# A hybrid SSD / gMLP decoder layer on one core: the first six projection tiles run on unnormalised features

## The chip, the cores and the metric

The kernel runs on one core of a Trainium2 chip. The time is the device time of one execution in microseconds (us), and the median of the runs is what counts.

## The reference

One layer of a decoder trunk works on 288 tokens (256 of a prompt and 8 samples of 4) of 2048 features, in float32. It normalises the tokens, projects them with one matrix whose columns are split among two groups of heads (a state-space group, SSD, with a short causal convolution in front of it, and a gated MLP that mixes positions), projects back, and runs a gated feed-forward block and an embedding gate. What the change touches is the beginning:

```python
def rmsnorm(x, g):
    y = xf * lax.rsqrt(jnp.mean(xf * xf, axis=-1, keepdims=True) + EPS)
    return (y * g.astype(jnp.float32)).astype(x.dtype)
...
n = rmsnorm(h, g_mix)
proj = n @ w_in
z, xbc, dt_raw, u, v = ...              # column ranges of proj
xbc_c, conv_new = causal_dwconv(xbc, conv0, conv_w, conv_b)
xbc_c = jax.nn.silu(xbc_c)
...
w = w_s[:, :Q, :Q] * jnp.tril(...)      # spatial weights of the gated MLP, masked
s = jnp.einsum('gts,bcsgd->bctgd', w, vr) + b_s
```

The factor of the norm is one number for each token, the gain `g` one for each feature.

## The kernel before

**Layout.** Features lie on the 128 partitions, tokens along the free axis: an activation is a list of 16 tiles of 128 x 288. A weight tile is 2048 x 128 (16 blocks of 128 x 128, 1 MB) and gives one output tile of 128 x 288 in PSUM. To keep float32 accuracy each operand is split into a high part in a reduced format and a low part, the rest; `mm3` (lines 175 to 181) makes three products for each block: high x high (line 179), low activation x high weight (line 180), high x low (line 181). One such set is called a triple here; a tile takes 16 of them.

**Splits.** `split` makes the two parts of an activation: `hi` on ScalarE with the gain as its scale (line 150), `lo` on VectorE (line 151). `split_w` does it for half a weight tile (8 blocks, 1024 columns): `whi` on ScalarE (line 172), `wlo` on VectorE (line 173), at a raised priority. `load` brings half a tile over SP's queue into one of four `raw` buffers; `whi` and `wlo` have three buffers each. `mtile` loads, splits and multiplies a whole tile into one of three `acc` buffers in PSUM; other results use five `pb` buffers.

**Start.** The features `xin` arrive in eight pieces of 288 KB, half over SP's and half over ScalarE's queue, and behind them the small tables. ScalarE squares each piece (line 239) and TensorE sums over features with a column of ones (`sum_tokens`, line 102). VectorE makes the reciprocal root in twelve small steps (lines 82 to 90), TensorE broadcasts it to all partitions (lines 118 and 120), and VectorE multiplies `xin` by it (line 249). Only then are the features split into `n_act`, which stays for all projection tiles. Tiles 0 to 2 are multiplied together, k by k, into `ps01`, with the narrow dt projection beside them (line 257, its weights `gw` multiplied by the gain at line 243).

**After it.** The loop at the end goes over four groups g of the SSD heads, with six convolution tiles each; for g = 0 these are the tiles 0 to 5. `dt_work` and `decay_work` turn the dt projection into decay factors when tile 0 is done. `conv_tile` copies a PSUM tile into `cbuf` on ScalarE (lines 331 and 332), and runs the convolution on both engines (lines 336 to 343); `cbuf` has three buffers, the others two. In groups 1 to 3, z tiles come between, and `advance` emits pieces of `ssd_group` of the group before. When the last group has ended, `mlp_pools` reuses its memory: GpSimd's queue loads the residual `h` again and then the spatial weights and biases, and line 576 multiplies the weights by the triangular mask `T1`. The sixteen tiles of the first part of the output projection follow, each added to `h` at line 707, then the rest of the v tiles, then `spatial` as a side job of the u tiles, which uses the masked weights in `mix` (line 597).

**Order.** The instructions are written in program order, and a scheduler at build time fixes the order on each engine from dependences, priorities (program order, but for the raised ones) and its own estimate of times; it may take a step far ahead of its place when its inputs are there. On the chip each engine then runs its list in that order.

## Time and profile before

| | us |
|---|---|
| median of 3 runs | 1802.67 (1802.15 to 1803.92) |
| the profiled execution | 1801.47 |
| its span in the trace | 1799.3 |
| TensorE busy | 1765.1 (98%) |
| VectorE busy | 1062.1 (59%) |
| ScalarE busy | 826.9 (46%) |

PE is TensorE, PEld its weight loads, DVE VectorE, ACT ScalarE, POOL GpSimd, SP SyncE. The granted clock of TensorE is given as a share of 2.4 GHz; 0.50 is its lower level, 1.2 GHz. A float32 matmul is recorded as two instructions. "Idle before" is the time for which an engine stood still just before an instruction, and after the arrow stands what it waited for. A busy TensorE is not one at its peak: only the clock and the count of products tell how fast it moves on.

### The profile page before, as it was taken

The numbers are of one execution on the slowest core, as the hardware profiler recorded it, in microseconds if no ns is written. First come the engines' busy times: TensorE is split into PE (matmuls) and PEld (weight loads), VectorE is DVE, ScalarE is ACT, GpSimd is POOL, SyncE is SP. The second block draws the span as 40 slices with busy tenths as digits, with TensorE's granted clock in tenths as the row PEclk, the third lists the DMA queues.
The fourth block names the chain that finished last, engine by engine and source line by source line (L and its number), as shares of the span: only waits on it lengthen the run. The fifth ranks groups of instructions, "written<-read, shape, count | busy, mean of one in ns | idle before, by whom it ended". The sixth has DMA issues, their size and how long they took to land.

```text
span 1799.3 us, 31672 instructions
## 1 busy us (share of the span) xinstructions
PE 1765.1 (98%) x13084; PEld 1731.5 (96%) x13084; DVE 1062.1 (59%) x1655; ACT 826.9 (46%) x1432; POOL 31.2 (2%) x79
## 2 busy tenths in 40 slices
PE   8999999998999999999999999999999999999996
PEld 7989988978999999999999999999999999999996
DVE  3768687776445686555555554444555555554665
ACT  3585758463345544444333333333333333444452
POOL 0001010101000000000000000000000000000000
PEclk6999999999999999999999999999999999999998
DMA  4536464627555544554555545555555455555452
GB/s 161 180 132 230 133 216 143 223 88 267 165 164 165 165 135 162 165 165 158 167 164 166 165 165 159 166 163 171 167 164 168 163 168 167 161 167 169 164 166 89
DMA packets 83600, 297.63 MB, mean 165 GB/s; under 512 B 9488, under 2 KB 9616, under 8 KB 83200
## 3 DMA queue, kind: packets, MB, share of 16 engines
q1 hardware_dynamic: 75600, 268.85, 46.3%
q0 software_dynamic: 6128, 23.34, 3.6%
q10 hardware_dynamic: 1728, 3.43, 0.5%
q8 instruction: 102, 1.67, 0.4%
q14 instruction: 42, 0.34, 0.1%
HBM read 283.19 MB, written 12.39 MB: 164 GB/s over the span
## 4 chain that ended last, share of the span: by engine, by line
PE 75%; DVE 0%; ACT 0%; DVEq 0%; issue 0%
PE acc L179 25%; PE acc L181 24%; PE acc L180 24%; PE pb L597 0%; PE pb L181 0%; PE pb L179 0%; PE pb L180 0%; PE pb L589 0%; DVE h L829 0%; PE pb L102 0%; PE pb L118 0%; DVE wlo L173 0%; DVE h L707 0%; PE pb L120 0%; DVEq L916 0%
## 5 line engine op out<-in xcount | busy, mean ns | idle before, releaser
L179 PE MATMUL acc<-hi,whi 128*128 128x288 f32 x4000 | 1187.5, 297 | 7.7 <-DVE h L707 4.4
L180 PE MATMUL acc<-lo,whi 128*128 128x288 f32 x4000 | 1184.9, 296 | 0.0
L181 PE MATMUL acc<-hi,wlo 128*128 128x288 f32 x4000 | 1181.0, 295 | 1.2 <-DVE wlo L173 1.2
L172 ACT CAST whi<-raw 128x1024 fp32r<-128x1024 f32 (+1 forms) x516 | 533.7, 1035 | 827.8 <-PE acc L180 664.8
L173 DVE TENSOR_TENSOR wlo<-raw,whi 128x1024 fp32r<-128x1024 f32 (+1 forms) x516 | 623.3, 1208 | 486.2 <-ACT whi L172 479.5
L179 PEld LDWEIGHTS acc<-hi,whi 128*128 128x128 f32 x4000 | 753.1, 188 | 11.7 <-issue 7.3
L181 PEld LDWEIGHTS acc<-hi,wlo 128*128 128x128 f32 x4000 | 755.0, 189 | 3.7 <-DVE wlo L173 1.8
L180 PEld LDWEIGHTS acc<-lo,whi 128*128 128x128 f32 x4000 | 753.8, 188 | 1.5 <-issue 0.6
L783 DVE SCALAR_TENSOR_TENSOR Up<-acc,rs 128x288 f32<-128x288 f32 x44 | 20.1, 457 | 41.9 <-PE acc L181 41.9
L778 DVE TENSOR_TENSOR G<-acc,rs 128x288 f32<-128x288 f32 x44 | 20.1, 457 | 41.6 <-PE acc L181 41.6
L338 DVE SCALAR_TENSOR_TENSOR cva<-cbuf,cwh,cva 128x312 f32<-128x312 f32 x72 | 38.5, 538 | 1.3 <-ACT cva L336 0.4
L551 ACT ACTIVATE gt<-gt 128x288 f32<-128x288 f32 x32 | 14.2, 443 | 40.5 <-DVE gt L550 40.5
L389 ACT ACTIVATE xw<-xdt,dec 128x64 f32<-128x64 f32 x96 | 24.4, 338 | 5.9 <-DVE xdt L386 5.9
L102 PEld LDWEIGHTS pss<-ones,sq 128*128 128x128 f32 x96 | 20.6, 333 | 3.9 <-ACT sq L239 3.9
L102 PE MATMUL pss<-ones,sq 128*128 128x1 f32 x96 | 20.6, 352 | 3.7 <-ACT sq L239 3.7
L418 DVE TENSOR_TENSOR h<-h,pb 128x512 f32<-128x512 f32 x32 | 20.9, 680 | 1.1 <-PE pb L417 1.1
L366 ACT ACTIVATE Rh<-cst,dtAh 128x128 fp32r<-128x128 f32 x64 | 20.6, 397 | 1.5 <-PE pb L371 1.5
L784 DVE TENSOR_TENSOR Up<-Up,G 128x288 f32<-128x288 f32 x44 | 20.2, 458 | 1.5
L366 ACT ACTIVATE Rl<-cst,dtAl 128x128 fp32r<-128x128 f32 x64 | 20.8, 399 | 0.0
L424 DVE TENSOR_TENSOR h<-h,decS 128x512 f32<-128x512 f32 x32 | 20.1, 683 | 0.0
L780 DVE SCALAR_TENSOR_TENSOR G<-Gt,G 128x288 f32<-128x288 f32 x44 | 19.9, 453 | 0.1
L779 ACT ACTIVATE Gt<-G 128x288 f32<-128x288 f32 x44 | 19.4, 441 | 1.2 <-DVE G L778 1.2
(270 smaller groups left out, 927.0 us busy)
## 6 DMA issues: line engine op xcount, KB each, us to landing
raw<-in_wa_dram SPq DMA_DIRECT2D x416, 512.0 KB, 3.6
raw<-in_wd_dram SPq DMA_DIRECT2D x64, 512.0 KB, 3.5
raw<-in_wd_dram SPq DMA_DIRECT2D x32, 384.0 KB, 3.1
h<-in_h0T_dram POOLq DMA_DIRECT2D x16, 512.0 KB, 6.6
out_dram<-h POOLq DMA_DIRECT2D x16, 512.0 KB, 5.9
h<-in_xT_dram POOLq DMA_DIRECT2D x4, 576.0 KB, 7.1
raw<-in_wple_dram SPq DMA_DIRECT2D x4, 512.0 KB, 3.6
xin<-in_xT_dram ACTq DMA_DIRECT2D x4, 288.0 KB, 6.0
```

Source lines behind the costliest of these rows:

```text
L102: nc.tensor.matmul(ps[:, c:c + 1], lhsT=acc[:, t:t + P], rhs=ones[:, 0:1], start=first and c == 0, stop=last and c == 2)
L172: nc.scalar.copy(a, r)
L173: nc.vector.tensor_sub(b, r, f32(a))
L179: nc.tensor.matmul(ps, lhsT=wh, rhs=hi, start=first, stop=False)
L180: nc.tensor.matmul(ps, lhsT=wh, rhs=lo, start=False, stop=False)
L181: nc.tensor.matmul(ps, lhsT=wl, rhs=hi, start=False, stop=last)
L338: nc.vector.scalar_tensor_tensor(ao, cb[:, j:j + NCO], wt[j], ao, op0=ALU.mult, op1=ALU.add)
L366: nc.scalar.activation(cols(r, i), T1, AF.Identity, scale=f32(d[:, c, k + i:k + i + 1]))
L389: nc.scalar.activation(xw[:, 64 * h:64 * h + 64], xd[:, 64 * h:64 * h + 64], AF.Identity, scale=dec[:, c, 8 * g + h:8 * g + h + 1])
L418: nc.vector.tensor_add(h0[q][:, i], h0[q][:, i], ps)
L424: nc.vector.tensor_mul(r3(hh, 64), r3(hh, 64), bc_in(decS[:, 2 * q + i, hs], 64))
L784: nc.vector.tensor_mul(u, u, G)
```

## The change

The first six tiles (group 0) are multiplied from `x_act`, the split of the features with the gain but without the norm. Since the norm is a factor of each token, it is applied to the output: `conv_tile` gets `rs0` and multiplies by it on VectorE as it copies from PSUM into `cbuf`, instead of the copies on ScalarE; `dt_work` does the same. The weights of tiles 0 to 2 are loaded and split in quarters (512 columns) in the order in which they are used, interleaved with `xin`; their second halves get buffers of their own in the start pool. The tables move from SP's and ScalarE's queues to GpSimd's, `vec` to the head of ScalarE's. The sums of squares are added up on VectorE (`sqa`), and TensorE sums once over features at the end (`rstd_compact`). Then `xin` is multiplied by the norm and split into `n_act` as before, for the tiles from group 1 on. The convolution's buffers move to a pool of their own, which is opened before the start pool. The multiplication of the spatial weights by the mask moves from `spatial_weights` into `spatial`, behind the reciprocal root `rv`.

```diff
@@ -211,6 +211,8 @@
     warm = small([P, 1], "warm")
     nc.gpsimd.memset(ones, 1.0)
     nc.scalar.activation(warm, ones[:, 0:1], AF.Exp)
+    cv_pool = tc.tile_pool(name="conv", bufs=1)
+    cvp = cv_pool.__enter__()
     start = tc.tile_pool(name="start", bufs=1)
     s0 = start.__enter__()
     xin = [s0.tile([P, 2, NT], F32, name=f"xin{q}") for q in range(8)]
@@ -223,39 +225,67 @@
     for _ in range(14):
         nc.tensor.matmul(wu[:, 0:P], lhsT=ones, rhs=ones, start=True, stop=True)
 
+    raws = {(m, j): st.tile([P, 1024], F32, tag="raw", name="raw", bufs=4) for j in range(2) for m in range(3)}
+
+    def first_w(m, j):
+        nc.sync.dma_start(raws[m, j // 2][:, 512 * (j % 2):512 * (j % 2) + 512],
+                          wa[m, :, 4 * j:4 * j + 4].rearrange("p k m -> p (k m)"))
+
+    nc.scalar.dma_start(vecs, vec)
     for q in range(8):
-        (nc.scalar if q % 2 else nc.sync).dma_start(xin[q], xT[:, 2 * q:2 * q + 2])
-    nc.sync.dma_start(vecs, vec)
-    nc.scalar.dma_start(csts, cst)
-    first = {(m, 0): load(wa[m, :, 0:8], 8) for m in range(3)}
-    nc.scalar.dma_start(wdts, wdt)
-    nc.scalar.dma_start(dtals, dtal)
-    nc.scalar.dma_start(scv, sconv)
-
-
-    pss = big("pss")
-    for q in range(8):
-        sq = s0.tile([P, 2, NT], F32, tag="sq", name="sq", bufs=4)
-        nc.scalar.activation(sq, xin[q], AF.Square)
-        for j in range(2):
-            sum_tokens(pss, sq[:, j], first=q + j == 0, last=q + j == 8)
-    halves = {at: split_w(raw, 8) for at, raw in first.items()}
-    nc.vector.tensor_mul(gw, wdts, bc_in(vecs[:, V_MIX:V_MIX + 16], 32))
-    rs0 = bcast_tokens(rsqrt_compact(pss[:, 0:3], 2048.0, EPS, "rm"), keep_psum=True)
-    n_act = []
+        (nc.scalar if q < 4 else nc.sync).dma_start(xin[q], xT[:, 2 * q:2 * q + 2])
+        if q % 2 == 0:
+            for m in range(3):
+                first_w(m, q // 2)
+    nc.gpsimd.dma_start(wdts, wdt)
+    nc.gpsimd.dma_start(csts, cst)
+    nc.gpsimd.dma_start(dtals, dtal)
+    nc.gpsimd.dma_start(scv, sconv)
+
+
+    def quarter(m, j):
+
+        if j % 2 == 0:
+            if j == 0:
+                w = [st.tile([P, 1024], F32R, tag=t, name=t) for t in ("whi", "wlo")]
+            else:
+                w = [s0.tile([P, 1024], F32R, name=f"{t}{m}") for t in ("whi", "wlo")]
+            halves[m, j // 2] = w
+        c = slice(512 * (j % 2), 512 * (j % 2) + 512)
+        w_hi, w_lo = halves[m, j // 2]
+        raw = raws[m, j // 2]
+        nc.scalar.copy(w_hi[:, c], raw[:, c])
+        nc.vector.tensor_sub(w_lo[:, c], raw[:, c], f32(w_hi[:, c]))
+
+    halves = {}
+    x_act, n_act = [], []
     ps01 = [big("ps01")[:, 0:NT] for _ in range(2)] + [pa.tile([P, NT], F32, tag="acc", name="acc")]
     pdt = big("pdt")
     for q in range(8):
+        for k in (2 * q, 2 * q + 1):
+            xk = xin[q][:, k % 2]
+            x_act.append(split(xk, gain=vcol(V_MIX, k)))
+            for m in range(3):
+                if k % 4 == 0:
+                    quarter(m, k // 4)
+                mm3(ps01[m], halves[m, k // 8], k % 8, x_act[k], k == 0, k == KD - 1)
+    nc.vector.tensor_mul(gw, wdts, bc_in(vecs[:, V_MIX:V_MIX + 16], 32))
+    for k in range(KD):
+        nc.tensor.matmul(pdt[32 * (k % 4):32 * (k % 4) + 32, 0:NT], lhsT=gw[:, k], rhs=xin[k // 2][:, k % 2],
+                         start=k < 4, stop=k >= 12, tile_position=(0, 32 * (k % 4)))
+
+    sqa = s0.tile([P, 2, NT], F32, name="sqa")
+    for q in range(8):
+        sq = sqa if q == 0 else s0.tile([P, 2, NT], F32, tag="sq", name="sq", bufs=1)
+        nc.scalar.activation(sq, xin[q], AF.Square)
+        if q:
+            nc.vector.tensor_add(sqa, sqa, sq)
+    nc.vector.tensor_add(sqa[:, 0], sqa[:, 0], sqa[:, 1])
+    rs0 = bcast_tokens(rstd_compact(sqa[:, 0], 2048.0, EPS, "rm"))
+    for q in range(8):
         nc.vector.tensor_mul(xin[q], xin[q], bc_mid(rs0, 2))
         for k in (2 * q, 2 * q + 1):
-            xk = xin[q][:, k % 2]
-            n_act.append(split(xk, gain=vcol(V_MIX, k), tags=LONG))
-            for m in range(3):
-                if (m, k // 8) not in halves:
-                    halves[m, 1] = split_w(load(wa[m, :, 8:16], 8), 8)
-                mm3(ps01[m], halves[m, k // 8], k % 8, n_act[k], k == 0, k == KD - 1)
-            nc.tensor.matmul(pdt[32 * (k % 4):32 * (k % 4) + 32, 0:NT], lhsT=gw[:, k], rhs=xk,
-                             start=k < 4, stop=k >= 12, tile_position=(0, 32 * (k % 4)))
+            n_act.append(split(xin[q][:, k % 2], gain=vcol(V_MIX, k), tags=LONG))
     nc.vector.tensor_scalar_mul(cwh, vecs[:, V_CB:V_CB + 120], 0.5)
 
     dt = small([P, 3, 32], "dt")
@@ -269,7 +299,7 @@
     decS = small([P, 8, 32], "decS")
     def dt_work():
         df = s0.tile([P, 384], F32, name="dtf")
-        nc.scalar.copy(df[:, 0:NT], pdt[:, 0:NT])
+        nc.vector.tensor_mul(df[:, 0:NT], pdt[:, 0:NT], rs0)
         nc.vector.tensor_copy(r3(df[:, NT:384], 32), bc_mid(df[:, 256:288], 3))
         pd = big("pd")
         for c in range(3):
@@ -322,14 +352,17 @@
     def samples(ap):
         return ap[:, 259:NCV].rearrange("p (b t) -> p b t", t=7)[:, :, 0:4]
 
-    def conv_tile(i, ps):
-        sd = sd_box["pool"]
-        cb, a, t = (sd.tile([P, NCV], F32, tag=n, name=n, bufs=b) for n, b in (("cbuf", 3), ("cva", 2), ("cvt", 2)))
+    def conv_tile(i, ps, rs=None):
+        cb, a, t = (cvp.tile([P, NCV], F32, tag=n, name=n, bufs=b) for n, b in (("cbuf", 3), ("cva", 2), ("cvt", 2)))
         nc.gpsimd.memset(cb[:, 0:3], 0.0)
         nc.scalar.copy(cb[:, 259:NCV].rearrange("p (b t) -> p b t", t=7)[:, :, 0:3], scv[:, i])
         new = cb[:, 259:NCV].rearrange("p (b t) -> p b t", t=7)[:, :, 3:7]
-        nc.scalar.copy(cb[:, 3:259], ps[:, 0:256])
-        nc.scalar.copy(new, r3(ps[:, 256:288], 4))
+        if rs is None:
+            nc.scalar.copy(cb[:, 3:259], ps[:, 0:256])
+            nc.scalar.copy(new, r3(ps[:, 256:288], 4))
+        else:
+            nc.vector.tensor_mul(cb[:, 3:259], ps[:, 0:256], rs[:, 0:256])
+            nc.vector.tensor_mul(new, r3(ps[:, 256:288], 4), r3(rs[:, 256:288], 4))
         ao, to = a[:, 0:NCO], t[:, 0:NCO]
         o = slab(name="cvo")
         wt = [cwh[:, 24 + 4 * i + j:25 + 4 * i + j] for j in range(4)]
@@ -573,13 +606,13 @@
         nc.gpsimd.dma_start(wss, wsS)
         nc.gpsimd.dma_start(w, wsT)
         nc.gpsimd.dma_start(b.rearrange("p a b -> p (a b)"), bsP[0:1].partition_broadcast(P))
-        nc.vector.tensor_mul(w, w, bc_mid(T1, KD))
         return bss, wss, w, b
 
     def spatial(nv, mp, bss, wss, w, b):
         vS = vS_box[0]
         sS = sS_box[0] = mp.tile([P, KD, 32], F32, name="sS")
         r = rstd_compact(nv.acc, 2048.0, 4.0 * EPS, "rv")
+        nc.vector.tensor_mul(w, w, bc_mid(T1, KD))
         vts = {}
 
         def to_tokens(g):
@@ -646,6 +679,7 @@
     def mlp_pools():
 
         sd_pool.__exit__(None, None, None)
+        cv_pool.__exit__(None, None, None)
         hp = ctx.enter_context(tc.tile_pool(name="hp", bufs=1))
         h = hp.tile([P, KD, NT], F32, name="h")
         mlp = tc.tile_pool(name="mlp", bufs=1)
@@ -669,7 +703,7 @@
         tiles = [16 + g, 20 + g] + list(range(4 * g, 4 * g + 4))
         zs = []
         for j, i in enumerate(tiles):
-            ps = ps01[at] if at < 3 else mtile(wa[at], n_act)
+            ps = ps01[at] if at < 3 else mtile(wa[at], n_act if g else x_act)
             if at == 0:
                 dt_work()
                 start.__exit__(None, None, None)
@@ -678,7 +712,7 @@
                 decay_work()
                 decay_sample()
             at += 1
-            conv_tile(i, ps)
+            conv_tile(i, ps, None if g else rs0)
             advance(1)
             if g and j in (1, 2, 4, 5):
                 zs.append(z_tile(mtile(wa[24 + 4 * (g - 1) + len(zs)], n_act)))
```

## Rows read from the trace of the kernel before

**Rows 1.** The page: TensorE's busy time, and the chain that ended last by engine

```profile
PE 1765.1 (98%) x13084; PEld 1731.5 (96%) x13084; DVE 1062.1 (59%) x1655; ACT 826.9 (46%) x1432; POOL 31.2 (2%) x79
...
PE 75%; DVE 0%; ACT 0%; DVEq 0%; issue 0%
```

**Rows 2.** Stretches: us, busy time and count by engine, granted clock, DMA share, GB/s

```profile
5.00:10.00 5.00, 2.21 (x11) 2.02 (x10) 0.00 (x0) 0.00 (x0) 0.00 (x0) 1.00 1.05 403
...
15.00:20.00 5.00, 5.00 (x25) 5.00 (x25) 2.45 (x2) 3.25 (x6) 0.00 (x0) 0.50 0.77 267
...
40.00:50.00 10.00, 10.00 (x83) 8.96 (x75) 7.94 (x19) 3.50 (x9) 0.00 (x0) 0.95 0.01 2
```

**Rows 3.** Timeline of the start: start us, duration, engine, line, operation, count, idle before

```profile
10.91 20.64 PE L102 MATMUL pss<-ones,sq 128*128 128x1 f32 x96 [3.69 <-ACT sq L239]
...
11.14 0.22 DVE L259 TENSOR_SCALAR cwh<-vec 128x120 f32<-128x120 f32 x1 [11.14 <-DMA vec<-in_vec_dram]
...
35.50 5.41 DVE L249 TENSOR_TENSOR xin<-xin,pb 128x576 f32<-128x576 f32 x8 [1.58 <-PE pb L120]
...
36.88 0.85 PE L179 MATMUL ps<-hi,whi 128*128 128x288 f32 x2 [1.42 <-ACT hi L150]
...
37.90 3.78 PE L257 MATMUL pdt<-xin,gw 128*32 128x288 f32 x32
...
41.61 0.40 PE L180 MATMUL ps<-lo,whi 128*128 128x288 f32 x1
```

**Rows 4.** Stretches, line 179 alone: the first product of each triple, counted

```profile
40.00:60.00 20.00, 11.64 (x41) 7.53 (x42) 0.97 0.33 110
...
60.00:80.00 20.00, 11.61 (x38) 7.77 (x38) 0.91 0.61 211
...
80.00:90.00 10.00, 7.40 (x26) 4.68 (x26) 1.00 0.47 172
```

**Rows 5.** DMA issues: KB each, median us from issue to landing

```profile
xin<-in_xT_dram ACTq DMA_DIRECT2D x4, 288.0 KB, 6.0
...
wsr<-in_wsT_dram POOLq DMA_DIRECT2D x1, 1024.0 KB, 12.6
```

**Rows 6.** Groups of instructions, 36 to 62 us: busy us, mean ns, idle before

```profile
L151 DVE SCALAR_TENSOR_TENSOR lo<-xin,vec,hi 128x288 fp32r<-128x288 f32 x16 | 7.0, 512 | 0.0
...
L249 DVE TENSOR_TENSOR xin<-xin,pb 128x576 f32<-128x576 f32 x8 | 5.4, 750 | 1.6 <-PE pb L120 1.6
```

**Rows 7.** Groups of VectorE's instructions, 50 to 100 us

```profile
L173 DVE TENSOR_TENSOR wlo<-raw,whi 128x1024 fp32r<-128x1024 f32 x15 | 18.3, 1221 | 12.8 <-ACT whi L172 12.8
...
L338 DVE SCALAR_TENSOR_TENSOR cva<-cbuf,cwh,cva 128x312 f32<-128x312 f32 x21 | 11.1, 537 | 0.7 <-ACT cva L336 0.4
...
L288 DVE SCALAR_TENSOR_TENSOR dtwt<-dtwt,dtws 128x96 f32<-128x96 f32 x7 | 1.8, 255 | 0.1
```

**Rows 8.** Timeline of TensorE, 68 to 72 us: the decay matmuls, first and last

```profile
68.34 0.33 PE L301 MATMUL pdec<-dtA,cst 128*128 128x64 f32 x2
...
69.94 1.97 PE L313 MATMUL pdec<-dtA,cst 32*128 32x32 f32 x16
```

**Rows 9.** Stretches, all engines: the first half of group 1

```profile
100.00:150.00 50.00, 50.00 (x365) 43.27 (x365) 37.70 (x70) 36.52 (x108) 1.39 (x5) 1.00 0.37 124
```

**Rows 10.** Timeline of VectorE, 432 to 436 us

```profile
432.09 2.29 DVE L576 TENSOR_TENSOR wsr<-wsr,cst 128x2048 f32<-128x2048 f32 x1 [5.00 <-DMA wsr<-in_wsT_dram]
...
434.30 1.18 DVE L707 TENSOR_TENSOR h<-h,acc 128x288 f32<-128x288 f32 x3
```

**Rows 11.** Stretches, line 179 alone: around the stop at 430 us

```profile
430.00:434.00 4.00, 0.00 (x0) 0.00 (x0) 0.95 0.66 275
...
434.00:438.00 4.00, 1.67 (x4) 1.28 (x4) 0.50 0.13 14
...
438.00:441.00 3.00, 1.88 (x6) 1.34 (x5) 0.59 0.75 246
```

**Rows 12.** TensorE's waits: us in total, times, longest us

```profile
PE acc L179 <- DVE h L707: 4.4, 1, 4.4
```

## Prediction

> **What bounds the kernel now.** I read the page's busy times first [rows 1]: TensorE is busy 1765.1 us of a span of 1799.3 us, and the chain that ended last is three quarters TensorE, nearly all of it the three products of each weight tile (lines 179 to 181). So time is won only where TensorE is idle or does work that the change drops. The table of stretches [rows 2] and the timeline of the start [rows 3] show where that is. The 48 sums of squares (96 records, line 102) hold TensorE from 10.91 us for 20.64 us; with the norm's own steps the first product is issued at 36.88 us, the 32 dt products (line 257) take the next 3.78 us, and only from 41.61 us do products run back to back. TensorE's clock is 0.50, its 1.2 GHz level, for most of this, although the engine is 100% busy from 15 to 20 us: being busy with one-column matmuls did not raise it. To follow position rather than busy time I count the first products of each triple (line 179; 16 a tile) by stretch [rows 4]. The 3 issued before 40 us [rows 3] and the 41 and 38 of the next two stretches of 20 us make 44 by 60 us and 82 by 80 us; 26 follow in 10 us. So the 48th (tiles 0 to 2) falls at 61.6 us, the 96th (start of tile 6) at 85.4 us, and a triple costs about 0.40 us, a tile 6.4 us. A second stop stands at 430 us (below).
>
> **Part 1: products from raw features.** Tiles 0 to 2 no longer wait for the norm. Their first product needs `vec`, `xin0` and three weight quarters, about 1.2 MB, and their splits. The DMAs moved 403 GB/s from 5 to 10 us [rows 2] and an `xin` piece landed 6.0 us after issue with eight in flight [rows 5]. I put the first triple at 8 us: 6 us if the first pieces land alone, 11 us if everything issued beside them (xin1 to 3, more quarters, and 1 MB of tables) lands together.
>
> Two hardware queues filled that stretch at 403 GB/s with all DMA engines busy (share 1.05), so a third queue cannot add bandwidth to it. The Trainium skill's page "DMA: Bandwidth & Descriptors", section "Issuing engines are not separate DMA queues", says the same and speaks against moving `wdt`, `cst`, `dtal` and `scv` to GpSimd's queue: they interleave with the pieces that the first product needs. By that rule my 8 us would be up to 2.6 us later (an estimate, 1.05 MB at the row's 403 GB/s).
>
> All 6.6 MB are in by about 19 us at that rate, counted from 2 to 3 us. The 48 triples take 48 x 0.40 = 19.2 us if TensorE is never short. Its suppliers: VectorE makes 16 `lo` in 7.0 us [rows 6] and 12 `wlo` quarters; a quarter, half of the 1.22 us of a 1024-wide one [rows 7], is 0.65 us with its fixed part, 7.8 us in all; 14.8 us together, below 19.2, and ScalarE the same. So TensorE sets the pace from 8 us to 27 us. I add 2 us for products at the low clock (0 to 5: a stretch at half clock costs half of itself): tiles 0 to 2 end at 29 us, 27 to 34.
>
> Behind them, on TensorE: the dt products, 3.8 us, which before filled a wait and now stand in the path; token sum and broadcast, 12 small matmuls at 0.12, 1.4 us (16 such take 1.97 us, [rows 8]). Then tiles 3 to 5, 19.2 us, and the dt and decay matmuls, 0.7 us (6 at 0.12) and 3.6 us (from 68.34 to 71.91, [rows 8]), which stood ahead of the 96th triple before too. Without any wait for another engine the 96th triple falls at 29 + 5.2 + 19.2 + 4.3 = 57.7 us, against 85.4.
>
> **Part 2: what VectorE must have done by then.** Tile 5 needs the PSUM buffer of tile 2, and so `rs0` and tile 2's eviction, now on VectorE; tile 6 needs tile 3's buffer and the first normalised features. In the order of the program the list is: main loop 14.8; `gw` 0.7; seven adds of squares and the fold, 5.1 (as a 576-wide product, 0.68); the reciprocal root 2.4 (twelve steps of three columns, 0.2 each, an estimate below the 0.25 of 96 columns); eight products with the norm 5.4 and 16 `lo` 7.0 [rows 6]; seven `wlo` of tiles 3 to 6 at 1.22, 8.5; four evictions of two instructions, 0.6 each, 2.4. That is 46.3 us. `dt_work` adds about 6 (23 small steps at 0.25, [rows 7]), and one convolution, whose buffer tile 3's eviction takes (three cyclic `cbuf`), 3 x 0.54 + 0.6 = 2.2: 54.5 us. From a start at 7 us without a gap this ends at 61.5 us; with 10% of gaps at 67 us. The squares and the adds fit into VectorE's spare 4 us of the main loop only in part. So VectorE, not TensorE, sets tile 6: 58 us if small steps and convolutions come late, 74 us if dt and three more convolutions are queued ahead and gaps are 10%. I take 62 us, nearest to the list without gaps. Gain at the 96th triple: 85.4 - 62 = 23 us (11 to 28). Evictions wait for `rs0`, and behind them on VectorE stand the `wlo` of the next tile and the first `lo` of tile 6; TensorE waits for both. The fall to half clock that such a wait brings is not added: before had one too, inside the 85.4.
>
> After tile 6 VectorE is some five convolutions, 11 us, behind its old position. From 100 to 150 us it was busy 37.7 of 50 us [rows 9], a slack of 12 us; three accumulators and three `cbuf` allow about that lag. I take 1 us of loss (0 to 5). If that slack were not there, up to 11 us would come back.
>
> **Part 3: covers.** ScalarE loses two eviction copies a tile and gains 16 `hi`; it stays beside the path, hidden by VectorE's longer list. The sixteen raw splits take 32 of 38 slabs until tile 5 ends and the six convolution outputs the other 6; no other slab is asked for in this group, so this costs nothing; a seventh claim would hold VectorE until tile 5 ends. On SP's queue the second halves of tiles 1 and 2 reuse two of the four `raw` buffers, so their quarters, and `xin5` to `xin7` behind them, wait until the first halves of tiles 0 and 1 are split, at about 11 us by the pace above. TensorE reaches the ninth k (their first use) at 8 + 8 x 1.2 = 17.6 us, and a landing takes up to 6 us [rows 5]: 0, to 3 us if it is late. The tables on GpSimd's queue come ahead of the states that `ssd_group` loads there much later, which wait for the start pool anyway: 0.
>
> **Part 4: the spatial mask.** Before, VectorE sat 5.0 us for `wsr` and then worked 2.29 us on the mask, with the adds of line 707 queued behind [rows 10]; the transfer took 12.6 us to land [rows 5]. TensorE ran at half clock after it [rows 11] and had waited 4.4 us for that add [rows 12]: 4 triples in the 8 us from 430 us where 20 fit. 6 more of 7.5 followed to 441 us [rows 11], so the stop cost 17.5 x 0.40 = 7 us. The mask is now issued after `rv`, behind the adds in program order, and its first use lies behind the sixteen output tiles and the rest of the v tiles. Even hoisted by the build's scheduler it stands behind the adds that are ready. Gain 7 us (0 to 7.5). In its new place it costs 2.3 us of VectorE's time beside TensorE: 0, or up to 2 if it delays the first `vt`.
>
> **Sum.** 23 - 1 + 7 = 29 us. Against the profiled execution, 1801.47 us (1799.3 of span and 2.2 around it): 1772.5. The median of the runs is 1.2 us above that execution: 1773.7, call it 1773.
>
> **The rivals.**
> Norm and convolutions first: VectorE's queue puts dt and convolutions ahead of tile 2's and 3's eviction, and tile 6 starts at 70 to 74 us with another fall of the clock. For it: in the old trace the eight norm products ran as one block from 35.50 us, ahead of every `lo` [rows 3]. Gain 9 to 14 in front, 16 to 21 in all: 1782 to 1787.
> Full cover: the squares hide in the main loop and the evictions come in time. Gain 27 and 7: 1766 to 1769.
> The mask does not move: the build's scheduler fills the same hole with it, since nothing but its transfer holds it back (in the old trace `cwh`, line 259, ran at 11.14 us, far ahead of its place, [rows 3]). The adds stay behind it: no 7 us, 1780.
> Slower: the start stays at 1.2 GHz. The clock stayed 0.50 through 100% busy stretches [rows 2], and after the stop at 430 us too it was 0.50 [rows 11]. If products arrive in small groups between waits for quarters, evictions and `rs0`, each triple costs 0.3 us more (about 0.7 us there, from 434.9 to 438 us, against 0.40). The Trainium skill's page "TensorE: Matmul & The Clock Gate", section "HAM oscillation — how this bites in real kernels", describes that: bursts between waits keep falling back to the low clock. The gain of 29 us is used up after 29 / 0.3 = 97 triples at the low clock, that is if tiles 0 to 5 all run so; with two tiles more (32 triples, 10 us) the time is 1812. Against it: at half clock a triple takes 0.7 us, longer than its supplies (0.3 us of VectorE's time), so products become dense, and dense products got 0.95 from 40 us on [rows 2].
>
> **How the numbers follow.** Forecast (1768 to 1780) 0.50; norm first 0.20; full cover 0.12; mask unmoved 0.10; slower 0.06; the rest, within 0.2%, where losses later eat the gain, 0.02. The range runs from the full cover with the first triple at 6 us and no low clock (2 us each, and 1 of rounding: 1761) to norm first with 4 us of the lag in group 1 given back (1791); outside are the slower case and the rest. A difference under 0.2% (3.6 us) can't be told from none here. Faster 0.92, same 0.02, slower 0.06.
>
> **What would show it.** In the new trace: first product at 6 to 11 us; the 48th triple near 29 us, the 96th near 62 us; VectorE over 90% busy from 10 to 65 us; a wait of TensorE on the new eviction into `cbuf` or on a `lo`; no wait on line 707's add near 400 us. It is wrong if the 96th triple is later than 74 us, if the clock stays 0.50 after 15 us, or if group 1 shows new waits on VectorE of over 5 us.

## The result, and the profile after

The median is 1785.37 us (1783.51 to 1786.97) against 1802.41 us (1801.66 to 1803.92) for the kernel before in the same runs: a ratio of 0.9904, 95% interval 0.9887 to 0.9921, 17.0 us faster. The forecast was 29 us faster; the time lies inside the range. The profiled execution of after took 1786.97 us, the slowest of its four, with a span of 1785.2 us: 14.1 us below the span of before, so the traces account for a little less than the medians.

The page of after, against [rows 1]: TensorE's busy time fell by 14.0 us, VectorE's rose by 13.0 us.

```profile
PE 1751.1 (98%) x12994; PEld 1713.6 (96%) x12994; DVE 1075.1 (60%) x1698; ACT 831.6 (47%) x1442; POOL 33.4 (2%) x83
...
PE 76%; DVE 0%; ACT 0%; DVEq 0%; issue 0%
```

Both kernels work through the same tiles in the same order, so a place in the work has a time in each. Place n is the start of the first product number 16 n (line 179, counted from 0). From place 6 on that is where tile n starts, as long as tiles have sixteen triples; the last row is a count alone. Up to place 5 the tiles run into one another (0 to 2 are multiplied k by k, and tile 3 begins among them), so there a place is a number of triples and not a tile. The table has the time of some places in each trace and the difference: what has been won up to there.

```
place    before    after   won
  0        36.9      8.1   28.8
  3        61.7     37.3   24.3
  5        79.6     52.2   27.4
  6        86.0     67.6   18.4
  9       107.7     86.9   20.8
 10       114.5     98.8   15.7
 17       175.0    161.3   13.7
 40       371.4    357.6   13.8
 46       434.9    420.7   14.2
 50       463.4    450.1   13.3
250      1755.6   1741.0   14.6
```

Three things are to be read from it. The products from raw features win 28.8 us at once; between places 5 and 6 a stop takes 9 us back; and from tile 17 on hardly anything moves any more, though the forecast had 7 us to come at tile 46. What goes between tiles 6 and 17 are for the most part the decay matmuls and the low clock after them, which before stood ahead of place 5 and now stand ahead of tile 10 (the last sixteen of them at 93.81 us, in place of the 69.94 of [rows 8]). The 18.4 us won at tile 6 thus hold some 5 us that are only put off.

The stretches of the start of after, with the columns of [rows 2]: us, busy time and count of PE, PEld, DVE, ACT and POOL, granted clock, DMA share, GB/s.

```profile
5.00:10.00 5.00, 2.32 (x14) 1.91 (x14) 1.96 (x5) 2.57 (x5) 0.00 (x0) 0.86 1.04 401
10.00:15.00 5.00, 5.00 (x19) 2.62 (x18) 4.59 (x9) 4.36 (x10) 0.00 (x0) 0.50 1.05 388
15.00:20.00 5.00, 5.00 (x35) 3.74 (x34) 4.93 (x11) 5.00 (x14) 0.00 (x0) 0.96 1.05 389
...
30.00:35.00 5.00, 5.00 (x40) 5.00 (x40) 2.25 (x3) 0.51 (x1) 0.00 (x0) 1.00 0.81 231
35.00:40.00 5.00, 5.00 (x40) 5.00 (x40) 1.95 (x12) 0.00 (x0) 0.00 (x0) 1.00 0.27 102
40.00:45.00 5.00, 5.00 (x41) 5.00 (x40) 1.27 (x2) 1.45 (x2) 0.00 (x0) 1.00 0.06 12
45.00:50.00 5.00, 5.00 (x40) 5.00 (x39) 5.00 (x8) 4.71 (x10) 0.00 (x0) 1.00 0.24 93
50.00:55.00 5.00, 2.60 (x20) 2.29 (x18) 5.00 (x16) 5.00 (x11) 0.00 (x0) 1.00 0.00 0
55.00:60.00 5.00, 2.33 (x10) 2.20 (x11) 5.00 (x12) 1.76 (x9) 0.00 (x0) 0.64 0.18 40
60.00:65.00 5.00, 5.00 (x29) 5.00 (x29) 4.98 (x11) 1.06 (x1) 2.12 (x4) 0.68 0.76 246
```

VectorE (third pair) is nearly full from 10 to 30 us, as forecast; then it works 5.5 of 15 us, while TensorE runs at its best; and from 45 us on VectorE is full and TensorE stands still for 5 of 10 us. What VectorE waits for in the hole shows in its timeline: start us, duration, engine, line, operation, count, and in brackets the idle time before it.

```profile
27.54 0.45 DVE L283 TENSOR_TENSOR sqa<-sqa 128x288 f32<-128x288 f32 x1
...
36.51 0.16 DVE L82 TENSOR_SCALAR rmx<-pb 128x3 f32<-128x3 f32 x1 [4.26 <-PE pb L102]
...
38.68 0.16 DVE L90 SCALAR_TENSOR_TENSOR rmy<-rmt,rmy 128x3 f32<-128x3 f32 x1
42.51 1.22 DVE L173 TENSOR_TENSOR wlo<-raw,whi 128x1024 fp32r<-128x1024 f32 x1 [3.66 <-ACT whi L172]
44.95 5.44 DVE L286 TENSOR_TENSOR xin<-xin,rs 128x576 f32<-128x576 f32 x8 [1.22 <-ACT rs L125]
```

On TensorE the two small steps of the norm's chain stand here:

```profile
35.75 0.72 PE L102 MATMUL pb<-ones,sqa 128*128 128x1 f32 x6
...
43.73 0.61 PE L118 MATMUL pb<-cst,rmy 128*128 128x128 f32 x4
```

The fold of the squares ends at 27.99 us, but the sum over features runs at 35.75; the root ends at 38.84, but its broadcast runs at 43.73. Both had their input for 5 to 8 us. TensorE was busy with products of the first tiles in between: the two steps stand behind these in its list, where the build's scheduler put them. So the norm products begin at 44.95 us.

TensorE's longest waits in after, for all of the span: us in total, times, longest.

```profile
PE pd L306 <- DVE dtf L303: 3.4, 1, 3.4
PE acc L181 <- DVE wlo L173: 3.2, 3, 1.5
PE acc L179 <- DVE h L741: 3.1, 1, 3.1
```

The first and half of the second are the stop at 52 us. The third is the wait of [rows 12], line 707 then and line 741 now: the stop at 430 us, which the moved mask was to remove, is still there. VectorE's timeline at that place:

```profile
417.87 2.29 DVE L615 TENSOR_TENSOR wsr<-wsr,cst 128x2048 f32<-128x2048 f32 x1 [3.73 <-DMA wsr<-in_wsT_dram]
420.08 1.18 DVE L741 TENSOR_TENSOR h<-h,acc 128x288 f32<-128x288 f32 x3
```

It is the pair of [rows 10] once more: the mask, whose new place in the program comes up some 180 us later (at 599 us, as an experiment below shows), has been put back directly ahead of the adds.

### The profile page after: what moved, and what is told of

Same layout as the page of the kernel before. It is cut to its first block, busy times and chain, and to the rows that moved or that the text cites. A ratio compares the mean times of both kernels' runs of the same rounds, so it can differ in the third digit from the quotient of the medians.

```text
span 1785.2 us, 31566 instructions
## 1 busy us (share of the span) xinstructions
PE 1751.1 (98%) x12994; PEld 1713.6 (96%) x12994; DVE 1075.1 (60%) x1698; ACT 831.6 (47%) x1442; POOL 33.4 (2%) x83
## 4 chain that ended last, share of the span: by engine, by line
PE 76%; DVE 0%; ACT 0%; DVEq 0%; issue 0%
PE acc L179 25%; PE acc L181 25%; PE acc L180 24%; PE pb L630 0%; PE pb L179 0%; PE pb L181 0%; PE pb L180 0%; PE pb L102 0%; PE pb L622 0%; DVE h L863 0%; PE pb L118 0%; DVE wlo L173 0%; DVE h L741 0%; PE pb L120 0%; DVEq L950 0%
## 5 line engine op out<-in xcount | busy, mean ns | idle before, releaser
L172 ACT CAST whi<-raw 128x1024 fp32r<-128x1024 f32 (+1 forms) x510 | 528.3, 1037 | 829.9 <-PE acc L180 657.6
L173 DVE TENSOR_TENSOR wlo<-raw,whi 128x1024 fp32r<-128x1024 f32 (+1 forms) x510 | 615.6, 1208 | 469.4 <-ACT whi L172 462.7
L157 DVE TENSOR_TENSOR lo<-Up,hi 128x288 fp32r<-128x288 f32 x44 | 19.9, 452 | 0.0
L156 ACT CAST hi<-Up 128x288 fp32r<-128x288 f32 x44 | 19.1, 434 | 1.2 <-DVE Up L818 0.5
```

The source lines that it names most:

```text
L172: nc.scalar.copy(a, r)
L173: nc.vector.tensor_sub(b, r, f32(a))
```

## The experiments

**The mask: moved line or moved work.** Does the line's new place do anything, and what is it worth when the mask really runs late? In the first kernel only the line is moved, in the kernel before.

```diff
-        nc.vector.tensor_mul(w, w, bc_mid(T1, KD))          # in spatial_weights
         r = rstd_compact(nv.acc, 2048.0, 4.0 * EPS, "rv")
+        nc.vector.tensor_mul(w, w, bc_mid(T1, KD))          # in spatial
```

> The kernel before with one part of the change alone: the product of the spatial weights with the mask is written behind the reciprocal root rv, nothing else. Theory: the line changes its place in the text, but nothing but its own transfer holds it back, so the scheduler at build time puts it back ahead of the adds of the output projection. Then TensorE waits about 4.4 us for those adds as before, and the time is that of before, 1802 us, within 0.2%. Rival (the prediction's part 4): the adds go first, TensorE does not stop, 7 us less, 1795 us.

Measured: 1803.4 us against 1802.66, ratio 1.0004 (0.9994 to 1.0014). VectorE's timeline of this run has the mask and the adds where they were:

```profile
431.02 2.29 DVE L582 TENSOR_TENSOR wsr<-wsr,cst 128x2048 f32<-128x2048 f32 x1 [4.13 <-DMA wsr<-in_wsT_dram]
433.23 1.18 DVE L707 TENSOR_TENSOR h<-h,acc 128x288 f32<-128x288 f32 x3
```

The second kernel is after with a mask that needs a value made from the root `rv` (a factor of 1), so that it cannot run before it.

```diff
-        nc.vector.tensor_mul(w, w, bc_mid(T1, KD))
+        keep = small([P, 1], "keep")
+        nc.vector.tensor_scalar(keep, r[:, 0:1], 0.0, 1.0, op0=ALU.mult, op1=ALU.add)
+        nc.vector.scalar_tensor_tensor(w, w, keep, bc_mid(T1, KD), op0=ALU.mult, op1=ALU.mult)
```

> The changed kernel, with the masked product made to depend on rv by a factor of 1 worked out from it, so that it cannot run before rv is there (about 600 us). Theory: the stop of TensorE at 413 us in the changed kernel is still the mask's wait for its weights on VectorE, with the adds queued behind it; without it 3.1 us of waiting and about 3 us at half clock go, 5 to 7 us in all: 1779 us against 1785. Rival: the adds then wait for something else that is as late (the residual h lands at about the same time as the weights, or a weight split is late): under 2 us of gain.

Measured: 1779.58 us (1777.10 to 1781.00), ratio 0.9870 (0.9855 to 0.9885). The adds run as soon as their tile is done, and the mask at 599 us:

```profile
416.65 1.18 DVE L743 TENSOR_TENSOR h<-h,acc 128x288 f32<-128x288 f32 x3 [2.90 <-PE acc L181]
...
599.39 2.34 DVE L617 SCALAR_TENSOR_TENSOR wsr<-wsr,keep,cst 128x2048 f32<-128x2048 f32 x1
```

What has been won at tile 50 rises from 13.3 to 19.0 us; 0.3 of the 5.7 was there at tile 40. A line moved alone did nothing; the dependence is worth 5.8 us by the medians.

**The stop at tile 6: order or amount of VectorE's work.** VectorE's list after 44.95 us has the norm products and the sixteen `lo` ahead of the first convolutions. This kernel is after with the norm products and the splits written behind the dt work and the first four convolutions (the decay work moves along).

```diff
+    def norm_acts():
         for q in range(8):
             ...
             if at == 0:
                 dt_work()
+            if at == 4:
+                norm_acts()
                 start.__exit__(None, None, None)
```

> The changed kernel, with the eight products with the norm and the sixteen splits of the normalised features written after the third tile's convolution and the dt work, not before them, so that VectorE has the dt copy and the low weight part of tile 5 ahead of most of the splits. Theory A (order): TensorE's stop from 52 to 58 us comes from two small steps that stand behind eleven splits on VectorE; with them ahead, the stop and the half clock after it go, and 5 to 8 us are won: 1778 to 1780 us. Theory B (VectorE is late as a whole, because it stood idle for about 9 us between 32 and 45 us while the norm's sum and broadcast waited in TensorE's list): the stop moves to tile 6, whose accumulator or features come no earlier, and the gain is 0 to 2 us.

Measured: 1789.53 us (1788.48 to 1791.09), ratio 0.9927 (0.9913 to 0.9942), 4 us slower than after, which neither theory had. The stop at 52 us is gone and another has come, as theory B had it; tile 6 starts at 67.5 us, as in after:

```profile
67.51 0.58 PE L179 MATMUL acc<-hi,whi 128*128 128x288 f32 x1 [8.13 <-ACT cvo L376]
```

The arrow names a copy on ScalarE; the second eviction of tile 3 ended 0.15 us before the product (more on that below). Behind the longer stop the clock is 0.50 from 65 to 70 us, where after has 1.00, and at tile 20 12.3 us are won in place of 13.8. So this other order does not bring tile 6 forward. The next two kernels take work and waits away. The first leaves out the squares, the sum, the root and the broadcast, and takes the norm's factor as 1.

```diff
-    sqa = s0.tile([P, 2, NT], F32, name="sqa")
-    ...
-    rs0 = bcast_tokens(rstd_compact(sqa[:, 0], 2048.0, EPS, "rm"))
+    rs0 = slab(name="rs", tag="rs")
+    nc.gpsimd.memset(rs0, 1.0)
```

> The changed kernel without the squares, their sum, the reciprocal root and the broadcast: the norm's factor is a constant 1, set at the start. What is left out is the value of the first norm. It takes away VectorE's idle time of 9 us between 32 and 45 us, and 5.6 us of adds and 2.4 us of the root on VectorE. Theory B (VectorE is late as a whole): the 96th triple comes 12 to 15 us earlier, at 53 to 56 us, and the time is 1770 to 1773 us. Theory A (order alone): the copy of dt and the weight part still stand behind the splits, TensorE stops as before, and no more than the 5.6 us of adds is won: 1779 us or more.

Measured: 1774.55 us (1772.08 to 1777.85), ratio 0.9845 (0.9830 to 0.9860). Tile 6 starts at 55.1 us, as theory B had it, and 27.8 us are won at tile 20; the time is 1.6 us above theory B's range and far below theory A's. The second keeps the squares and their additions and leaves out only sum, root and broadcast:

```diff
-    rs0 = bcast_tokens(rstd_compact(sqa[:, 0], 2048.0, EPS, "rm"))
+    rs0 = slab(name="rs", tag="rs")
+    nc.gpsimd.memset(rs0, 1.0)
```

> The kernel after with the squares and their eight additions kept, but the sum over features, the root and the broadcast left out: the norm's factor is the constant 1, so the output is that of unscaled features. It tells the two halves of what the norm costs VectorE at the start apart: the additions (7 by 0.75 us and one of 0.45, 5.7 us) and the idle time (4.3 us in front of the root, 3.7 in front of the weight rests and 1.2 in front of the norm products, 9 us). Theory 'idle time': tile 6's first product comes at 55 to 60 us (without any of the norm's chain it came at 55.1, in the kernel after at 67.6) and the time is 1774 to 1778 us. Theory 'work': the additions are what costs, tile 6 comes at 61 to 67 us and the time is 1780 to 1785 us.

Measured: 1774.02 us (1772.98 to 1777.33), ratio 0.9849 (0.9832 to 0.9865); tile 6 at 57.8 us, 22.1 us won at tile 20. The place of tile 6 speaks for the idle time. The median lies in that theory's range too, but by help of something else: the scheduler put the mask behind the first adds here, at 412.90 us, so that 27.3 us are won at tile 50 (28.2 without the additions), and without these 5 us the time would fall between the two theories. At tile 20 the 14.0 us between after and the kernel without the norm's chain fall apart into 5.7 us, as much as the additions take on VectorE, and 8.3 us for sum, root and broadcast, near VectorE's 9.1 us of idle time in its three holes. Of the 8.3 us, 2.0 are there at place 3 already, ahead of the holes' effect on tile 6. The 8.3 us are also more than waiting: the root's twelve steps take VectorE 2.3 us, and with the factor known from the start the norm products, the evictions (from 42.33 us on in place of 50.68) and the dt steps run earlier too. So the chain of sum, root and broadcast costs at least as much as the additions; how much of it is the wait for TensorE alone these runs do not separate.

**Can the chain be made shorter on VectorE?** The next kernel has the late mask and a root on all partitions: one matmul with a 128 x 128 matrix of ones, the root's steps 288 wide, no broadcast.

```diff
-    rs0 = bcast_tokens(rstd_compact(sqa[:, 0], 2048.0, EPS, "rm"))
+    tot = big("tot")[:, 0:NT]
+    nc.tensor.matmul(tot, lhsT=ones, rhs=sqa[:, 0], start=True, stop=True)
+    rx, rt = sqa[:, 1], slab(name="rt", tag="ta")
+    ...                              # the root's steps, 288 wide
```

> The kernel after with the mask truly late (as in the run mask_late), and with the norm's chain cut shorter: one matmul against a 128x128 matrix of ones leaves the sum of squares on all partitions, and the root is taken 288 wide on VectorE, nine instructions of some 0.42 to 0.51 us (the 288-wide ones took 0.45) in place of eleven narrow ones of 0.16, with no broadcast matmuls and no copy on ScalarE. In the kernel after the root ended at 38.8 us and its broadcast was run only at 43.7, behind products in TensorE's list; the norm products began at 44.95. Theory 'idle time': the root ends at 40 to 41 us, the norm products begin at 40.5 to 42, tile 6's first product comes at 63 to 65 us in place of 67.6, and the time is 1775 to 1777 us against 1779.6 for the late mask alone. Rival: the nine wide instructions (4 us) take the place of the idle time, and the time stays within 1.5 us of 1779.6.

Measured: 1782.60 us (1782.35 to 1783.12), ratio 0.9890 (0.9876 to 0.9905): 3 us slower than the late mask alone. Neither range held. The root has twelve wide steps, as many as the narrow one, and not the nine (and eleven) of the expectation: ten of 0.46 us and two of 0.31. The sum still comes late, and a weight rest that waited for `whi` stands between the eighth step and the ninth, so the norm products begin at 45.23 us, no earlier than in after:

```profile
35.01 0.46 DVE L288 TENSOR_SCALAR sqa<-tot 128x288 f32<-128x288 f32 x1 [2.98 <-PE tot L285]
...
40.88 1.23 DVE L173 TENSOR_TENSOR wlo<-raw,whi 128x1024 fp32r<-128x1024 f32 x1 [2.26 <-ACT whi L172]
...
45.23 3.43 DVE L296 TENSOR_TENSOR xin<-xin,rs 128x576 f32<-128x576 f32 x5
```

(The window cuts the last block; it has eight products.) So this kernel did not make the chain shorter, and is no test of what a shorter one would bring. The 3 us go at tile 6: TensorE stands 7.1 us in one piece in front of it, and the clock is 0.50 and 0.61 from 65 to 75 us, where the late mask alone had 1.00; from tile 6 to tile 7 what has been won falls from 18.1 to 15.3 us (18.7 to 18.6 with the late mask alone).

**Three of the eight norm products on GpSimd**, with the late mask:

```diff
-        nc.vector.tensor_mul(xin[q], xin[q], bc_mid(rs0, 2))
+        (nc.gpsimd if q >= 5 else nc.vector).tensor_mul(xin[q], xin[q], bc_mid(rs0, 2))
```

> The kernel after with the mask truly late (as in the run mask_late), and with three of the eight norm products (of 0.75 us each on VectorE, the last three) on GpSimd. Theory 'VectorE's list as a whole sets tile 6': 2.2 us less in the list, tile 6's first product comes 1.5 to 2.5 us before 67.6 and the time is 1777 to 1778.5 us. Rival: the products on GpSimd end later than VectorE's would have, or slow VectorE's own instructions, the splits of the last three pairs come late, and the time is 1779 to 1784 us.

Measured: 1783.30 us (1781.46 to 1785.23), ratio 0.9894 (0.9879 to 0.9909), 3.7 us slower than the late mask alone; tile 6 at 70.3 us. The rival held. Groups from 40 to 60 us (busy us, mean ns, idle before), first of after, then of this run:

```profile
L286 DVE TENSOR_TENSOR xin<-xin,rs 128x576 f32<-128x576 f32 x8 | 5.4, 752 | 1.2 <-ACT rs L125 1.2
```

```profile
L286 DVE TENSOR_TENSOR xin<-xin,rs 128x576 f32<-128x576 f32 x5 | 7.2, 1494 | 1.2 <-ACT rs L125 1.2
...
L286 POOL TENSOR_TENSOR xin<-xin,rs 128x576 f32<-128x576 f32 x3 | 5.8, 1971 | 41.1 <-ACT rs L125 41.1
```

Five products beside GpSimd took VectorE longer (7.2 us) than eight alone (5.4).

**The tables beside the features.** After with the four tables issued last on SyncE's queue in place of GpSimd's:

```diff
-    nc.gpsimd.dma_start(wdts, wdt)      # and csts, dtals, scv
+    nc.sync.dma_start(wdts, wdt)        # and csts, dtals, scv
```

> The kernel after with the four tables (dt weights, constants, dt A, convolution state) issued from SyncE's queue behind the features and the first weights, in place of GpSimd's queue beside them; nothing else is changed. If the queues share the DMA engines, the first features and weights land sooner: theory 'shared', the first product comes 0.5 to 2.6 us before the 8.1 us of the kernel after, and the features that come last (xin of the upper half) 1 to 3 us sooner. Rival 'not shared': the first product stays within 0.3 us of 8.1. In both the time stays within 3 us of 1785.4, as VectorE's list sets tile 6: the dt products move from the places 2 to 24 of the main loop to place 24, and the sum of squares from 46 to 52, which can cost 1 to 2 us.

Measured: 1785.21 us (1784.45 to 1787.06), ratio 0.9906 (0.9891 to 0.9921), the time of after. The first product comes at 7.9 us in place of 8.1, as the rival had it; the upper half of the features lands at 12.4 to 16.5 us in place of 15.3 to 18.9, as the theory had it. DMA issues (KB each, median us to landing), first of after, then of this run:

```profile
xin<-in_xT_dram ACTq DMA_DIRECT2D x4, 288.0 KB, 8.7
```

```profile
xin<-in_xT_dram ACTq DMA_DIRECT2D x4, 288.0 KB, 6.2
```

and this run's stretches, beside the first two of after above:

```profile
5.00:10.00 5.00, 4.06 (x20) 3.34 (x20) 2.73 (x6) 3.23 (x7) 0.00 (x0) 1.00 1.04 399
10.00:15.00 5.00, 4.01 (x25) 3.20 (x25) 4.94 (x9) 4.87 (x10) 0.00 (x0) 1.00 1.06 384
```

The rate is the same (399 and 384 GB/s against 401 and 388), and the clock is 1.00 in both stretches. The 17th triple starts at 16.8 us in place of 21.8 and the 49th at 31.5 in place of 37.3. Most of that is not the transfers' doing, but that of the dt products, whose place in TensorE's list changed as well: the list of after has them in groups among the first triples, twenty of the 32 records ahead of the 17th; here they run in one block behind the 24th. First after, then this run:

```profile
10.46 1.18 PE L274 MATMUL pdt<-xin,gw 128*32 128x288 f32 x4
...
16.49 0.68 PE L274 MATMUL pdt<-xin,gw 128*32 128x288 f32 x4
```

```profile
19.57 2.15 PE L274 MATMUL pdt<-xin,gw 128*32 128x288 f32 x32
```

Counted from the start of a record to the start of the next, the dt products hold TensorE for 5.9 us up to the 49th triple in after and for 2.1 us here. That is 3.8 of the 5.6 us by which the way from the first product to the 49th triple is shorter; 1.4 us are the triples themselves, and 0.6 us the norm's sum, which comes later here. The expectation had the move of the dt products down as a cost; no run moved them alone. But tile 6 waits for VectorE all the same: TensorE stands 8.5 us in front of it, and of the 5.8 us won at place 3, 1.2 are left at tile 20.

**What tile 6 waits for at the end of VectorE's list.** In after the first product of tile 6 follows the second eviction of tile 3 (end 67.46 us) by 0.15 us, and the same distance stands in nact4, wide_root, late_pool and tables_sp, at 65.0 to 70.3 us:

```profile
67.28 0.18 DVE L365 TENSOR_TENSOR cbuf<-acc,rs 128x32 f32<-128x32 f32 x1
...
67.60 0.37 PE L179 MATMUL acc<-hi,whi 128*128 128x288 f32 x1 [0.87 <-DVE cbuf L365]
```

Tile 6 takes tile 3's accumulator, and tile 3 can be evicted when tile 0 gives its `cbuf` back. The next kernel has the late mask and a fourth `cbuf`.

```diff
-    for n, b in (("cbuf", 3), ("cva", 2), ("cvt", 2))
+    for n, b in (("cbuf", 4), ("cva", 2), ("cvt", 1))
```

> The kernel after with the mask truly late (as in the run mask_late), and with four buffers in place of three for the convolution's input (cbuf), paid for by one in place of two for the tanh (cvt). In the kernel after, in nact4, in late_pool and in wide_root tile 6's first product follows the second eviction of tile 3 (VectorE, cbuf<-acc) by 0.15 us: there are three accumulators, tile 6 takes tile 3's, and tile 3 can be evicted only when one of the three cbuf is free, which tile 0 gives back after its three convolution steps on VectorE (62.4 to 66.8 us). Theory 'accumulator': with a fourth cbuf tile 3 is evicted before the convolution steps, tile 6's first product comes at 60 to 63.5 us in place of 67.3, and the time is 1774 to 1777 us against 1779.6. Rival 'list as a whole': tile 6 comes early, but the convolution steps that are behind on VectorE hold up tiles 7 to 10 by as much; at tile 20 the gain over the kernel before stays within 1.5 us of the 14.1 of mask_late, and the time is 1778 to 1780.5 us.

Measured: 1778.01 us (1776.86 to 1779.53), ratio 0.9863 (0.9848 to 0.9878), 1.6 us under the late mask alone and just inside the rival's range. Tile 3 is evicted at 60.05 us and the 0.87 us are gone, but the stop at 52 us, which has nothing to do with the accumulator, stays (3.43 us for `dtf`), and tile 6 starts at 64.9 us. At tile 20 15.9 us are won against 14.1, 1.8 more where the rival had at most 1.5; 1.0 of it was there at place 1 already, before the buffer can matter. Alone the buffer is worth 0.8 to 1.8 us.

**Both together:** late mask, fourth `cbuf`, tables on SyncE's queue.

> The run cbuf4 with the four tables on SyncE's queue as in tables_sp, where tiles 1 and 2 began 5 us sooner than in the kernel after and the gain at tile 20 was 15.0 us against 13.8. Theory 'accumulator': both add up, tile 6 at 58 to 62 us, time 1772.5 to 1776 us. Rival 'list as a whole': 1777 to 1779.5 us, 1 us under the late mask alone.

Measured: 1774.08 us (1772.83 to 1774.81), ratio 0.9838 (0.9822 to 0.9855): the fastest version with all of the computation in it, 11.3 us below after and 28.5 below before. Tile 6 starts at 58.9 us, and place and time are those of the theory; 18.6 us are won at tile 20 and 24.1 at tile 50. By place: the tables alone (with the dt products that moved along) had brought 1.2 us at tile 20 and the buffer at most 1.8; together they bring 4.5 over the late mask. With the tables moved alone TensorE stood 8.5 us in front of tile 6, here 1.1 us: triples that are done early are of use only where accumulators come free early too.

## Why the prediction was right, and where it was not

**First product, first tiles.** Forecast 8 us, measured 8.05. The 48 triples should end at 29 us and the 49th start behind 5.2 us of small work, at 34; it started at 37.3. From start to start, the way there holds 21.9 us of triples (forecast 19.2 and 2 for the low clock), 5.9 us of dt products (forecast 3.8), 0.6 us of the norm's sum and 1.0 us of waits. So the term of the dt products was too small: their 32 records (16 products, and not the 32 of the text) ran in groups of four among the triples, two of the groups at half clock. Between 10 and 15 us TensorE was 100% busy at clock 0.50, with 19 instructions where 35 fit in the next stretch: one such stretch, as I had allowed, but a whole one. The Trainium skill's page "DMA: Bandwidth & Descriptors", section "Issuing engines are not separate DMA queues", says that transfers issued by different engines interleave on the same DMA engines; the traces agree for the features on ScalarE's queue (8.7 us to landing beside the tables, 6.2 without them). It bore not on the first product, where I had applied it (0.2 us), but on the pieces behind it.

**VectorE sets tile 6: right; its 61.5 us: wrong.** The sum had 54.5 us of work from 7 us on without a gap, or with 10% of gaps 67 us. From 7.00 to 67.46 us the trace has 49.18 us of work and 11.3 us of gaps, 19%:

```profile
7.00:67.46 60.46, 52.63 (x338) 45.59 (x338) 49.18 (x102) 36.31 (x75) 2.32 (x6) 0.89 0.56 193
```

The work was over-estimated by 5 us (the small dt steps mostly ran behind tile 6), and the gaps are the step that failed. I had costed the token sum and the broadcast by their 1.4 us on TensorE and had not asked when TensorE's list lets them run. They ran 7.8 and 4.9 us after their inputs were there, and VectorE, which had nothing else that was ready, stood. No run moved these two steps forward in TensorE's list, as a raised priority might, so what their place alone costs stays open. The gain at tile 6 was 18.4 us in place of 23.

**After tile 6.** I had taken 1 us of loss; it was 4.6 (18.4 at tile 6, 13.8 at tile 20). VectorE's lag is not the cause: from 100 to 150 us it was busy 39.8 of 50 us, and TensorE busy throughout. The sum had put the decay matmuls ahead of the 96th triple in both kernels; after has them, with their fall of the clock, behind tile 9.

**The mask: wrong.** 7 us were forecast and none came. The step that failed is "even hoisted by the build's scheduler it stands behind the adds that are ready": it was hoisted, and it stood ahead of them. My rival "the mask does not move" was what happened, and I gave it 0.10. The size was nearly right: where the mask could not be hoisted it brought 5.8 us. In sum the forecast's 23 - 1 + 7 became 18.4 - 4.6 + 0 by the traces; the time stayed inside the range, but not in the 1768 to 1780 us that I had held likeliest.

**The rivals.** The rival "norm and convolutions first" gave 1782 to 1787 us, and 1785.4 lies in it. Half of its mechanism held: the norm products did run as one block and tile 3's eviction did stand behind a convolution. But tile 6 came at 67.6 us and not at 70 to 74, the one other order that was tried was no faster (nact4), and the rival counted the mask's gain in: that its time is met is partly luck. "Full cover" fell. The start at the low clock fell too: from 15 to 55 us the clock was 0.96 to 1.00, though behind the stop at 52 us the low level came back for a while (0.64 and 0.68 from 55 to 65 us); as the Trainium skill's page "TensorE: Matmul & The Clock Gate", section "HAM oscillation — how this bites in real kernels", has it, a wait was followed by products at half clock, but for a stretch and not for whole tiles.

## What to carry to other kernels

A step that is moved in the program has moved only if the built list shows it; where the place matters, make it depend on something that is late (0 us for the line, 5.8 us for the dependence). The same holds the other way round: a table moved to another queue also moved the products that use it in TensorE's list, so compare the order of instructions before a gain is put down to the transfers. Where a short step of a dependent chain is put on the busiest engine, price its place in that engine's list, not its length: 1.4 us of sum and broadcast stood for 12.7 us in TensorE's list with their inputs there. And where the start of a pipeline is bound by one supplier, earlier work ahead of it and more buffers behind it brought little each and more together (1.2 and at most 1.8 us alone, 4.5 together).

## What the runs showed of the hardware

- GpSimd and VectorE, each multiplying float32 tiles of 128 x 576 from two SBUF inputs at the same time, slow each other: VectorE's mean rose from 752 (after) to 1494 ns (late_pool). The Trainium skill's page "SBUF — State Buffer", section "Who interferes with whom", says that a VectorE instruction with two SBUF inputs contends with a GpSimd instruction that reads SBUF; these rows agree, and give the price: three products on GpSimd cost more of VectorE's time than they took off it.
- With DMA at 384 to 401 GB/s in both, 1.0 MB of tables on a third queue made the features on ScalarE's queue land 8.7 us after issue in place of 6.2; it did not change the rate.
- The 32 records of the dt products held TensorE for 2.1 us in one block at clock 1.00; in groups of four among the full-width products, two groups at half clock, they held it for 5.9 us. What makes a group dear these runs do not show.
- TensorE was 100% busy at its 1.2 GHz level from 10 to 15 us in after, and at 2.4 GHz with gaps (busy 4.01 of 5 us) in the same stretch of tables_sp. What it did before differs: in after it was busy 2.32 of the 5 us ahead, in tables_sp 4.06.
